# Values of four heads at a time in the first mixer: 512 moving columns in place of 256

## The chip, the cores and the metric

The kernel runs on one core of a Trainium2 chip. The metric is the device time of one execution in microseconds (us); the time before is the median of three runs, 1239.77 us (1239.33 to 1240.48). The program is a two-layer decoder trunk in fp32: a gated linear recurrence (HGRN2) with eight heads, a gated convolutional feed-forward block, a differential attention, a second feed-forward block, over 512 tokens of 1024 features. Only the recurrence, the first fifth of the time, is touched by the change.

Engines are named as in the profile: PE is the matrix engine (PEld its weight loads), DVE the vector engine, ACT the scalar engine, POOL the general one, SP the engine that issues most transfers.

## The reference, cut to what matters

```python
def hgrn2_mixer(h, w_in, w_out, g_norm, lb):
    proj = h @ w_in
    q, f, i, g = jnp.split(proj, ...)          # i: the values, 8 heads of 128
    q = jax.nn.silu(q)
    log_f = jnp.logaddexp(jnp.log(lb), jnp.log1p(-lb) + jax.nn.log_sigmoid(f))
    k = -jnp.expm1(log_f)
...
        o_intra = jnp.einsum('bthk,bshk,btshk,bshv->bthv', qb, kb, decay, vb)
        S_new = jnp.exp(b_last)[..., None] * S + jnp.einsum('bshk,bshv->bhkv', k_dec, vb)
...
    o = rmsnorm(o, g_norm) * jax.nn.silu(g)
    return o @ w_out
```

(The score and value products are written as one here.) The values `i` are a projection of the normed input like q, f and g, and they are needed with tokens on the partitions, 128 tokens in each tile.

## The kernel before, in words

**Products.** Every fp32 product is made of three matmuls of split operands (`mm3`, L97 to L101): high by high, high by low and low by high. A weight tile of 128x1024 is loaded by SP into one of three staging buffers (`stage`, L81), then split: ACT writes the high part (L59), DVE the low part (L60). The parts have three buffers each (`whi`, `wlo`). A projection `proj` onto 128 features takes 24 matmuls: eight slices of the input, three each, with the weights as the stationary operand and 512 tokens moving.

**Values.** The function `value` makes the values of 128 tokens (index j). Here the split input is stationary and the weight columns move. Before the change a call covers two heads: 256 columns, eight slices, three matmuls each. `values(qt)` makes four such calls for head pair qt, from two weight tiles, and writes each result with the row scale into a quarter of the tile `vt` (L332, ACT).

**One head on its way.** `prep` (L339 to L414) turns the f and q projections into scaled queries and keys; its work is on DVE, with copies on ACT. Keys have six buffers, which is one head's worth (`KB`); queries have seven (`QB`), four of them used by a head. `intra` then runs on PE in three pieces:

- scores: small matmuls L424 to L438 of 16 to 80 columns into the banks `pa` and `pb`, and three transposes (L446). The first key of the next head (L347, DVE) reuses the buffer that L424 reads, so it waits for these.
- state: L451, three matmuls with the values.
- output: L491 and L493. L491 needs the masked scores: DVE copies them by masks (L469, the last one is L480), then ACT copies them into place (L483, L486, L488). This chain from the scores to L488 is called the score chain below.

`readout` gates the output with the g projection. Head h's output is "output h" below, its scores are "scores h".

**Order.** The opening `begin` is written out by hand: the f, q and g projections of head 0, then the values of the first two token tiles while the row scales are worked out. The rest of the mixer is ordered by the framework's scheduler, from the loop at the end of `hgrn`: each engine has one fixed list of instructions, which it works off in order. PSUM has four banks `mm` for projections and values, and four banks `at` for the pieces of `intra`.

## Time and profile before

| what | value |
|---|---|
| median of three runs | 1239.77 us (1239.33 to 1240.48) |
| the profiled execution's own time | 1239.78 us |
| its span | 1237.8 us, so 2.0 us lie around it |
| PE busy | 99% of the span |
| DVE busy | 68% of the span, 191.14 us of the 230 us from 20 to 250 us |
| ACT busy | 47% of the span |
| granted PE clock | 1.0 in all stretches of the mixer |

The matmul durations in the profile are from start to modelled end and overlap each other. What a matmul costs in a packed stream is read from the distance of starts: in the stream from 30.15 us to 35.91 us 48 matmuls of 256 columns start, 0.120 us each, though each is listed with 0.28 us. DVE durations overlap by some 0.08 us in the same way.

The scores of heads 0 to 7 start at 46.91, 75.43, 102.07, 124.94, 146.30, 179.19, 200.56 and 221.96 us.

### The profile page before, as it was taken

To read this page: it belongs to the slowest core of one execution; us is meant where nothing else is said; L and a number is where in the kernel's file an instruction comes from. 1 tells how busy PE (TensorE), PEld (TensorE's weight loads), DVE (VectorE), ACT (ScalarE), POOL (GpSimd) and SP (SyncE) were. 2 spreads that over 40 slices of the span, in tenths; PEclk is the share of its full clock that TensorE was granted. 3 is DMA by queue.
4 is the path that set the end of the run, shared out by engine and by line. 5 is a ranking of instruction groups with operands and counts; after the bars stand their busy time and mean duration, and the time that the engine had idled before them with its cause. 6 is when DMAs were issued, how large, how long until landed. Compare 5 with 4: busy or idle time off the path is not lost.

```text
span 1237.8 us, 18004 instructions
## 1 busy us (share of the span) xinstructions
PE 1226.9 (99%) x6994; PEld 1040.4 (84%) x6994; DVE 841.6 (68%) x1643; ACT 578.5 (47%) x1007; POOL 10.1 (1%) x32
## 2 busy tenths in 40 slices
PE   9999999999999999999999999999999999999997
PEld 8888898888888888888888989888888888888887
DVE  7988989587777777633356887877687777762333
ACT  6564555354444444422345666655444444442223
POOL 0000000000000000000000000000000000000001
PEclk9999999999999999999999999999999999999998
DMA  6234232132333333233323322322233333323322
GB/s 233 69 87 122 86 86 57 64 119 86 102 102 91 97 102 90 90 96 100 103 86 116 90 80 75 102 69 86 88 100 102 91 97 102 94 85 97 103 81 69
DMA packets 39613, 117.46 MB, mean 95 GB/s; under 512 B 4280, under 2 KB 10216, under 8 KB 39528
## 3 DMA queue, kind: packets, MB, share of 16 engines
q1 hardware_dynamic: 38488, 115.37, 30.5%
q8 instruction: 55, 0.90, 0.3%
q10 hardware_dynamic: 1040, 0.94, 0.2%
q14 instruction: 30, 0.25, 0.1%
HBM read 112.09 MB, written 3.68 MB: 94 GB/s over the span
## 4 chain that ended last, share of the span: by engine, by line
PE 67%; issue 30%; DVE 1%; ACT 1%; DMA 0%; POOL 0%; SPq 0%; POOLq 0%; ACTq 0%; DVEq 0%
PE mm L99 19%; PE mm L101 19%; PE mm L100 19%; PE po L1021 1%; PE sc L978 1%; PE sc L977 1%; PE tp L1008 1%; PE sc L99 1%; PE sc L100 1%; PE at L491 1%; PE sc L101 1%; PE at L424 1%; PE at L493 0%; PE at L451 0%; DMA raw<-in_w_fqg_dram 0%
## 5 line engine op out<-in xcount | busy, mean ns | idle before, releaser
L99 PE MATMUL mm<-xh,whi 128*128 128x512 f32 x944 | 370.7, 393 | 0.5 <-ACT whi L59 0.4
L100 PE MATMUL mm<-xl,whi 128*128 128x512 f32 x944 | 368.7, 391 | 0.5 <-DVE xl L63 0.5
L101 PE MATMUL mm<-xh,wlo 128*128 128x512 f32 x944 | 367.7, 390 | 0.0
L60 DVE TENSOR_TENSOR wlo<-wst,whi 128x1024 fp32r<-128x1024 f32 (+1 forms) x172 | 206.0, 1200 | 146.1 <-ACT whi L59 144.3
L59 ACT CAST whi<-wst 128x1024 fp32r<-128x1024 f32 (+1 forms) x172 | 177.1, 1033 | 245.8 <-PE mm L100 205.7
L99 PEld LDWEIGHTS mm<-xh,whi 128*128 128x128 f32 x944 | 177.4, 188 | 37.2 <-ACT whi L59 1.1
L101 PEld LDWEIGHTS mm<-xh,wlo 128*128 128x128 f32 x944 | 177.2, 188 | 37.1 <-DVE wlo L60 0.2
L100 PEld LDWEIGHTS mm<-xl,whi 128*128 128x128 f32 x944 | 177.4, 188 | 36.9 <-DVE xl L63 2.0
L99 PE MATMUL mm<-hh,whi 128*128 128x512 f32 (+1 forms) x374 | 141.0, 377 | 0.0
L100 PE MATMUL mm<-hl,whi 128*128 128x512 f32 (+1 forms) x374 | 140.8, 377 | 0.0
L101 PE MATMUL mm<-hh,wlo 128*128 128x512 f32 (+1 forms) x374 | 140.8, 376 | 0.0
L680 DVE TENSOR_TENSOR u<-mm,rbc_f 128x512 f32<-128x512 f32 x88 | 60.2, 688 | 73.1 <-PE mm L101 73.1
L100 PEld LDWEIGHTS mm<-hl,whi 128*128 128x128 f32 x374 | 70.4, 188 | 13.0
L101 PEld LDWEIGHTS mm<-hh,wlo 128*128 128x128 f32 x374 | 70.4, 188 | 13.0
L99 PEld LDWEIGHTS mm<-hh,whi 128*128 128x128 f32 x374 | 70.4, 188 | 12.7
L59 ACT CAST hh<-c 128x512 fp32r<-128x512 f32 x44 | 27.3, 620 | 103.1 <-DVE c L691 103.1
L682 ACT ACTIVATE c<-u,pack 128x512 f32<-128x512 f32 x88 | 71.5, 817 | 8.1 <-DVE u L680 4.3
L99 PE MATMUL mm<-whi,xh 128*128 128x256 f32 x248 | 71.5, 288 | 0.0
L101 PE MATMUL mm<-whi,xl 128*128 128x256 f32 x248 | 70.3, 283 | 0.0
L100 PE MATMUL mm<-wlo,xh 128*128 128x256 f32 x248 | 70.1, 283 | 0.0
L684 DVE SCALAR_TENSOR_TENSOR c<-u,pack,c 128x512 f32<-128x512 f32 x88 | 66.1, 751 | 2.7
L683 DVE SCALAR_TENSOR_TENSOR c<-u,pack,c 128x512 f32<-128x512 f32 x88 | 65.4, 745 | 0.0
(283 smaller groups left out, 1686.3 us busy)
## 6 DMA issues: line engine op xcount, KB each, us to landing
wst<-in_w_up_dram SPq DMA_DIRECT2D x88, 512.0 KB, 3.6
wst<-in_w_down_dram SPq DMA_DIRECT2D x32, 512.0 KB, 3.5
wst<-in_w_fqg_dram SPq DMA_DIRECT2D x21, 512.0 KB, 3.7
wst<-in_w_kq_dram SPq DMA_DIRECT2D x16, 512.0 KB, 3.6
wst<-in_w_down_dram SPq DMA_DIRECT2D x16, 384.0 KB, 3.2
wst<-in_w_i_dram SPq DMA_DIRECT2D x8, 512.0 KB, 4.0
wst<-in_w_ao_dram SPq DMA_DIRECT2D x8, 512.0 KB, 4.5
wst<-in_w_v_dram SPq DMA_DIRECT2D x8, 512.0 KB, 3.7
```

Source lines behind the costliest of these rows:

```text
L59: i = nc.scalar.copy(hi, x)
L60: j = nc.vector.tensor_tensor(lo, x, hi.bitcast(F32), ALU.subtract)
L99: mm(out, s[0], m[0], start=start, stop=False)
L100: mm(out, s[0], m[1], start=False, stop=False)
L101: mm(out, s[1], m[0], start=False, stop=stop)
L424: mm(pa[row, c * P:c * P + 80], ks[1][:, st], r1[:, :, 8 * bk:8 * bk + 8], start=True, stop=True, tile_position=(0, 32 * g))
L491: mm(ch(po, j), vh(j), sct[:, j], start=True, stop=(j == 0))
L680: v.tensor_tensor(u[:, 2:], ps, rb, ALU.mult)
L682: s.activation(c, u[:, 2:], AF.Identity, bias=self.cb[:, layer, n:n + 1], scale=w(2))
L683: v.scalar_tensor_tensor(c, u[:, 1:T + 1], w(1), c, ALU.mult, ALU.add)
L684: v.scalar_tensor_tensor(c, u[:, 0:T], w(0), c, ALU.mult, ALU.add)
L977: mm(sc[c], qs[h][:, c, oi], ks[h][0][:, c, 0:n], start=True, stop=False)
```

## The change

The values are made for four heads at a time. The weights `w_i` are packed in halves of 512 columns instead of quarters of 256, four weight tiles of 128x1024 for a half, so a call of `value` streams 512 columns and fills a whole bank. There are two halves instead of four quarters; `values(half, js)` is called for two token tiles ahead of the `intra` of the head before, and for two after it, at h = 0 and h = 4. The fourth weight tile of a half is split into the buffers `spare`, which before served a later tile alone. Each result has a tile of its own, 128x512, out of six buffers. `begin` stages three value tiles instead of two and the first weights of head 1, and does only the first four input slices of its two token tiles. The query tiles have five buffers instead of seven.

```diff
-KB, QB = 6, 7
+KB, QB = 6, 5
...
-        staged = [self.stage(src) for src in (a["w_i"][0, 0], a["w_i"][0, 1], a["w_fqg"][3])]
+        staged = [self.stage(a["w_i"][0, n]) for n in range(3)]
...
-            nxt = self.weight_split(staged[2])
+            ws.append(self.weight_split(staged[2]))
             values = [self.bank("mm"), self.bank("at")]
-            self.value(values[0], xs, ws, 0, range(KD))
+            self.value(values[0], xs, ws, 0, range(KD // 2))
             rb = self.rows(rc, "n0", "at")
-            self.value(values[1], xs, ws, 1, range(KD))
+            self.value(values[1], xs, ws, 1, range(KD // 2))
...
-            hi, lo = ws[k // 4]
-            c = slice((k % 4) * 256, (k % 4) * 256 + 256)
-            self.mm3(ps[:, :256], (xs[k][0][:, tk], xs[k][1][:, tk]), (hi[:, c], lo[:, c]), k == 0, k == KD - 1)
+            hi, lo = ws[k // 2]
+            c = slice(k % 2 * T, k % 2 * T + T)
+            self.mm3(ps, (xs[k][0][:, tk], xs[k][1][:, tk]), (hi[:, c], lo[:, c]), k == 0, k == KD - 1)
...
+            def values(half, js):
+                if js[0] == 0:
+                    for n in range(len(w_i) % 4, 4):
+                        w_i.append(self.weights(a["w_i"][half, n], tiles=spare if n == 3 else None))
+                for j in js:
+                    begun_j = half == 0 and j < 2
+                    ps = begun[j] if begun_j else self.bank("mm")
+                    self.value(ps, xs, w_i[-4:], j, range(KD // 2 if begun_j else 0, KD))
+                    vt[half, j] = hp.tile([P, T], F32, tag="vt", name="vt", bufs=6)
+                    s.activation(vt[half, j], ps, AF.Identity, scale=rc[:, j:j + 1])
...
-                if h % 2 == 0:
-                    vt[h // 2] = values(h // 2)
+                if h % 4 == 0:
+                    values(h // 4, (0, 1))
                 if h:
-                    o[h - 1] = keep(h - 1, intra(h - 1, vt[(h - 1) // 2], *pr.pop(h - 1)))
+                    o[h - 1] = keep(h - 1, intra(h - 1, *pr.pop(h - 1)))
+                if h % 4 == 0:
+                    values(h // 4, (2, 3))
```

The scheduler's lists change with it, up to the end of the mixer; behind it PE's list is the same as before. Three places matter below.

PE before, at output 0. In a row, the tile left of the arrow is written; right of it stand the moving and the stationary operand. `whi,xh` with 128x256 is a value matmul, `xh,whi` with 128x512 one of a projection.

```order
L99 MATMUL mm<-whi,xh_265 128x256
L100 MATMUL mm<-wlo,xh_265 128x256
L101 MATMUL mm<-whi,xl_266 128x256
L99 MATMUL mm<-whi,xh_143 128x256
L100 MATMUL mm<-wlo,xh_143 128x256
L491 MATMUL at<-scd_394,vt 128x128 x2
L493 MATMUL at<-q_470,S 128x128
...
L101 MATMUL mm<-whi,xl_144 128x256
L99 MATMUL mm<-whi,xh_163 128x256
```

PE now, at the same place:

```order
L101 MATMUL mm<-xh_253,wlo 128x512
L99 MATMUL mm<-xh_265,whi 128x512
L100 MATMUL mm<-xl_266,whi 128x512
L491 MATMUL at<-scd_370,vt 128x128 x2
L493 MATMUL at<-q_446,S 128x128
...
L424 MATMUL at<-r_622,k_616 32x80
L426 MATMUL at<-r_638,k_634 32x48
```

Between scores 0 and output 0 PE had 48 projection matmuls and 26 value matmuls of 256 columns; now it has 71 projection matmuls. The 70 value matmuls that followed output 0 are gone from here, and scores 1 (L424) follow it at once.

DVE before, at the last masked copy (L480) of head 1's scores; `sd` is the masked copy, `F`, `suf`, `tot`, `su` are tiles of `prep` for head 3:

```order
L469 COPY_PREDICATED sd_397<-mask,at 128x4x4
L412 TENSOR_TENSOR tot_910<-tot_902 128x4
L344 TENSOR_SCALAR F<-sf,om,lb 128x512
L480 COPY_PREDICATED sd_397<-mask,at 128x4x16
L364 TENSOR_TENSOR suf<-F 128x128
L365 TENSOR_TENSOR suf<-F,suf 128x128
```

DVE now, at the same place:

```order
L357 TENSOR_TENSOR r_1123<-r_1123,F 128x128
L498 TENSOR_TENSOR ge<-mm,rbc_n_348 128x512
L469 COPY_PREDICATED sd_373<-mask,at 128x4x8
L386 TENSOR_TENSOR su_1146<-tot,su_1146 128x32
L358 TENSOR_TENSOR r_1123<-r_1123,F 128x128
L60 TENSOR_TENSOR wlo<-wst,whi 128x1024
L359 TENSOR_TENSOR r_1123<-r_1123,F 128x128
L469 COPY_PREDICATED sd_373<-mask,at 128x4x4
L387 TENSOR_TENSOR tot_1147<-tot,su_1146 128x32
L501 TENSOR_TENSOR gg<-ge,sg 128x512
L360 TENSOR_TENSOR r_1123<-r_1123,F 128x128
L480 COPY_PREDICATED sd_373<-mask,at 128x4x16
```

Head 3's `prep` up to L387 and a gate (L498, L501) now stand ahead of the last masked copy of head 1. From head 1's L347 up to this L480, DVE's list has 115 rows where it had 99: one more each of L349, L356 to L360, L364 to L366, L385 to L387, L498 and L501, and two more of L354 (one of head 3, and that of head 1, which stood just ahead of L347).

ACT before, in the opening (`rbc` is the tile of row scales, with which the prep of head 0 starts):

```order
L307 ACTIVATE om<-dl 128x8
L59 CAST whi<-wst 128x1024 x2
L332 ACTIVATE vt<-mm,rcol_n_299 128x256
L198 COPY rbc_n_360<-at 128x512
L341 ACTIVATE sf<-fe 128x512
```

ACT now, at the same place:

```order
L307 ACTIVATE om<-dl 128x8
L59 CAST whi<-wst 128x1024 x2
L59 CAST spare_96<-wst 128x1024
L198 COPY rbc_n_348<-at 128x512
L341 ACTIVATE sf<-fe 128x512
```

The split of the fourth value tile stands ahead of the copy of the row scales, where the first eviction of values stood.

More of the change, by code (lines that the diff above doesn't have):

```diff
@@ L272, in begin @@
             proj_tail(2)
-            nxt = self.weight_split(staged[2])
+            ws.append(self.weight_split(staged[2]))
             values = [self.bank("mm"), self.bank("at")]
-            self.value(values[0], xs, ws, 0, range(KD))
+            self.value(values[0], xs, ws, 0, range(KD // 2))
             rb = self.rows(rc, "n0", "at")
-            self.value(values[1], xs, ws, 1, range(KD))
-        return rb, rc, ws, values, nxt
+            self.value(values[1], xs, ws, 1, range(KD // 2))
+        return rb, rc, ws, values
     def value(self, ps, xs, ws, j, ks):
@@ L297, in hgrn @@
             f_ps, q_ps, g_ps = (self.bank() for _ in range(3))
-            rb, rc, w_i, begun, w_f = self.begin(xs, acc, (f_ps, q_ps, g_ps), raw)
+            rb, rc, w_i, begun = self.begin(xs, acc, (f_ps, q_ps, g_ps), raw)
             yt[0] = hp.tile([P, 3, 2, T], F32R, tag="y0", name="y0")
@@ L316, in big, with project @@
                 return hp.tile([P, T], F32, tag=tag, name=name, bufs=bufs)
-            def project(n, w=None):
-                w = w or self.weights(a["w_fqg"][n])
+            def project(n):
+                w = self.weights(a["w_fqg"][n])
                 ps = self.bank("mm")
@@ L322, in project @@
                 return ps
-            def values(qt):
-                ws = w_i if qt == 0 else [self.weights(a["w_i"][qt, n]) for n in range(2)]
-                vt = hp.tile([P, 4, 256], F32, tag="vt", name="vt", bufs=2)
-                for j in range(4):
-                    ps, ks = self.bank("mm") if qt or j > 1 else begun[j], range(KD)
-                    if qt == 0 and j < 2:
-                        ks = ()
-                    self.value(ps, xs, ws, j, ks)
-                    s.activation(vt[:, j], ps[:, :256], AF.Identity, scale=rc[:, j:j + 1])
-                return vt
+            def values(half, js):
[8 more added lines that the diff above has]
+                    s.activation(vt[half, j], ps, AF.Identity, scale=rc[:, j:j + 1])
             def prep(h, f_ps, q_ps):
@@ L415, in prep, with intra @@
                 return r1, r2, qs, ks, tt
-            def intra(h, vt, r1, r2, qs, ks, tt):
+            def intra(h, r1, r2, qs, ks, tt):
                 mm = nc.tensor.matmul
@@ L441, in intra @@
                 ch = lambda t, c: t[:, c * P:(c + 1) * P]
-                vh = lambda j: vt[:, j, (h % 2) * P:(h % 2 + 1) * P]
+                vh = lambda j: vt[h // 4, j][:, h % 4 * P:(h % 4 + 1) * P]
                 q128, k128 = qs[128], ks[128]
@@ L517, in hgrn @@
                 if h:
-                    f_ps, q_ps = project(3 * h, w_f if h == 1 else None), project(3 * h + 1)
+                    f_ps, q_ps = project(3 * h), project(3 * h + 1)
                 pr[h] = prep(h, f_ps, q_ps)
@@ L531, in hgrn @@
             readout(NH - 2, o[NH - 2], gg[0])
-            o[NH - 1] = keep(NH - 1, intra(NH - 1, vt[3], *pr.pop(NH - 1)))
+            o[NH - 1] = keep(NH - 1, intra(NH - 1, *pr.pop(NH - 1)))
             readout(NH - 1, o[NH - 1], gg[1])
@@ L1207, in by_quarter, with by_half @@
     return np.ascontiguousarray(w.reshape(2, 4, P, 4, 256).transpose(3, 0, 2, 1, 4).reshape(4, 2, P, 1024))
+def by_half(w):
+    return np.ascontiguousarray(w.reshape(4, 2, P, 2, T).transpose(3, 0, 2, 1, 4).reshape(2, 4, P, 1024))
 def score_mask():
@@ L1254, in pack @@
         "w_fqg": fqg,
-        "w_i": by_quarter(iv),
+        "w_i": by_half(iv),
         "w_ao": by_tile(i["a_w_out"][0]),
```

## The prediction

> **What bounds the kernel now.** I begin with the head of the page: the span, the busy shares, the granted clock and the chain that ended last.
>
> ```profile
> span 1237.8 us, 18004 instructions
> PE 1226.9 (99%) x6994; PEld 1040.4 (84%) x6994; DVE 841.6 (68%) x1643; ACT 578.5 (47%) x1007; POOL 10.1 (1%) x32
> PEclk9999999999999999999999999999999999999998
> PE 67%; issue 30%; DVE 1%; ACT 1%; DMA 0%; POOL 0%; SPq 0%; POOLq 0%; ACTq 0%; DVEq 0%
> ```
>
> The reader should see one engine in use all the time, at full clock, and a chain that is PE's own work and issue for 97%. So the time is the sum of the distances between PE's starts, plus the few places where PE waits. The change touches the mixer, up to about 250 us, and behind it PE's list is unchanged. The windows (columns: stretch, its length, then PE, PEld, DVE, ACT, POOL busy) narrow it down:
>
> ```profile
> 20.00:250.00 230.00, 229.16 (x2168) 201.02 (x2168) 191.14 (x509) 120.80 (x255) 0.23 (x3) 1.00 0.28 84
> ```
>
> PE is idle for 0.84 us in 230, DVE is busy 83% of it. A change here pays only by fewer PE microseconds, and can lose by making PE wait for DVE.
>
> **Term 1: the columns.** The groups up to 400 us, split by shape, count the value matmuls (one line of the three), and the timeline of PE gives the spacing of starts:
>
> ```profile
> L101 PE MATMUL mm<-whi,xl 128*128 128x256 f32 x120 | 34.1, 284 | 0.0
> L101 PE MATMUL at<-whi,xl 128*128 128x256 f32 x8 | 2.3, 282 | 0.0
> ```
>
> ```profile
> 14.36 0.39 PE L99 MATMUL mm<-xh,whi 128*128 128x512 f32 x1
> ...
> 18.44 0.39 PE L99 MATMUL mm<-xh,whi 128*128 128x512 f32 x1
> ...
> 30.15 0.28 PE L99 MATMUL mm<-whi,xh 128*128 128x256 f32 x1
> ...
> 35.91 0.40 PE L99 MATMUL mm<-xh,whi 128*128 128x512 f32 x1
> 36.15 0.40 PE L100 MATMUL mm<-xl,whi 128*128 128x512 f32 x1
> ...
> 41.38 0.39 PE L99 MATMUL mm<-xh,whi 128*128 128x512 f32 x1
> ```
>
> 128 in each of three lines makes 384 matmuls of 256 columns. From 30.15 to 35.91 us two token tiles' values start, 48 matmuls in 5.76 us: 0.120 us each. For 512 columns, 18 projection matmuls lie between 14.36 and 18.44 us, 0.227 each, and 24 between 35.91 and 41.38, 0.228 each. The change makes 192 matmuls of 512 columns out of the 384, with the same kinds of operand. Before: 384 x 0.120 = 46.1 us. After: 192 x 0.2275 = 43.7 us. **Gain 2.4 us** (2.3 to 2.5 by the two spacings). The listed durations (0.284 against 0.39) would give 34 us, and are the wrong numbers: they overlap. The two spacings fit a fixed part of 12 to 13 ns a matmul, and halving the number of matmuls saves 192 of these.
>
> The Trainium skill ("TensorE: Matmul & The Clock Gate", section "Back-to-back issue gap") gives an isolated gap of N/2.4 + 2.5 ns, that is 109 ns for 256 columns and 216 ns for 512; an estimate by it puts the gain at 0.5 us instead. The trace disagrees at both sizes (120 and 227 ns), so the fixed part is taken from the trace.
>
> **Term 2: the one wait.** All of PE's idle time behind 20 us lies at output 0:
>
> ```profile
> 46.91 0.37 PE L424 MATMUL at<-r,k 128*32 128x80 f32 x8
> ...
> 50.88 0.48 DVE L347 TENSOR_SCALAR k<-sn,om 128x512 f32<-128x512 f32 x1
> ...
> 62.76 0.23 DVE L480 COPY_PREDICATED sd<-mask,at 128x64 f32<-128x64 int32 x1
> ...
> 64.19 0.28 PE L100 MATMUL mm<-wlo,xh 128*128 128x256 f32 x1
> 64.84 0.36 ACT L488 COPY scd<-at 64x256 f32<-64x256 f32 x1
> 65.31 0.68 PE L491 MATMUL at<-scd,vt 128*128 128x128 f32 x4 [0.83 <-issue]
> ...
> 66.86 0.36 PE L101 MATMUL mm<-whi,xl 128*128 128x256 f32 x1
> 67.06 0.28 PE L99 MATMUL mm<-whi,xh 128*128 128x256 f32 x1
> ```
>
> The profile calls the 0.83 us "issue", but L491 starts 0.11 us after ACT's last copy of the scores ended (65.20). PE waited for the score chain: its next start came 1.12 us after the last one instead of 0.12, so the wait cost **1.0 us**. The stretch from scores 0 to output 0 lasted 18.40 us, 17.4 without the wait. The order shows that the 26 value matmuls in it (3.1 us) give way to 23 more projection matmuls (5.2 us), and that eight of the 32 smallest matmuls move ahead (0.2 us): 17.4 - 3.1 + 5.2 - 0.2 = 19.3 us of PE work as cover. The chain needs 18.3 us, and less now, since L354 (1.1 us) no longer stands ahead of L347. The wait goes, 1.0 us gained.
>
> **Term 3: what is late next.** The cover is not thicker everywhere. Output 0 is now followed at once by scores 1, so DVE has to finish heads 1 and 2 sooner. I sum from scores 0 to output 1.
>
> ```profile
> 75.43 0.37 PE L424 MATMUL at<-r,k 128*32 128x80 f32 x8
> ...
> 93.76 0.60 PE L491 MATMUL at<-scd,vt 128*128 128x128 f32 x4
> ...
> 120.79 0.36 ACT L488 COPY scd<-at 64x256 f32<-64x256 f32 x1
> 121.37 0.61 PE L491 MATMUL at<-scd,vt 128*128 128x128 f32 x4
> ```
>
> ```profile
> 50.90:89.20 38.30, 33.71 (x101) 1.00 0.24 69
> ```
>
> ```profile
> L354 DVE TENSOR_TENSOR r<-qe,sq__1224 128x512 f32<-128x512 f32 x1 | 1.1, 1079 | 0.0
> ...
> L356 DVE TENSOR_TENSOR r<-r,F 128x256 f32<-128x256 f32 x8 | 5.3, 662 | 0.1
> ...
> L349 DVE TENSOR_TENSOR qe<-mm,rbc_n 128x512 f32<-128x512 f32 x8 | 5.5, 683 | 0.0
> L498 DVE TENSOR_TENSOR ge<-mm,rbc_n 128x512 f32<-128x512 f32 x8 | 5.5, 690 | 0.0
> L501 DVE TENSOR_TENSOR gg<-ge,sg 128x512 f32<-128x512 f32 x8 | 5.7, 718 | 0.0
> ...
> L360 DVE TENSOR_TENSOR r<-r,F 128x128 f32<-128x128 f32 x8 | 3.1, 389 | 0.1
> L387 DVE TENSOR_TENSOR tot<-tot,su 128x32 f32<-128x32 f32 x8 | 1.7, 210 | 0.2
> ```
>
> PE: 19.3 us to output 0, 1.55 us for the output itself (65.31 to 66.86), then scores 1 to output 1. That took 18.33 us (75.43 to 93.76) with 66 projection matmuls and will hold 96, of them 30 new: 18.33 + 30 x 0.228 = 25.2. Together 46.0 us.
>
> DVE: before, head 1's L347 started 3.97 us behind scores 0; without L354 ahead of it 2.9. From there to head 1's L480 DVE was busy 33.7 us (the window). The list now has 16 more instructions: two L354 (2.2), L356 (0.66), four of 0.39 (like L360), three more of the same 128x128 size (1.2), three of 0.21 (like L387), and L349, L498, L501 (2.1), 8.3 us by durations. They overlap by some 0.08 us each, so 7.0 to 8.3; I take 7.6. Then 2.4 us of copies (62.76 to 65.20): 2.9 + 33.7 + 7.6 + 2.4 = 46.6 us. DVE is late by 0.6 us, if it is never idle on the way; were L347 to start as soon as its operands allow, nearer 2.5 us, it is nearly in time. Between no wait and the 4.6 us by which this stretch was longer than its busy time before (38.3 - 33.7), the sum is nearest to the low end: **a wait of 0.5 us** at output 1. Of the later outputs, 2, 3, 6 and 7 lose 1 to 4 us of cover by the order. Output 2 had the least to spare (0.22 us, 121.15 to 121.37); it loses 1.0 us, but head 3's prep, which DVE did in between, now lies earlier (at output 1, the rows above). I cost them at nothing, and leave up to two waits of 1.0 us for them to a rival.
>
> **Edits that cost nothing, and their cover.** Weight traffic stays at eight value tiles of 512 KB, moved in SP's list, and splits stay at eight. The fourth tile's split now stands ahead of the row scales on ACT:
>
> ```profile
> 22.65 4.94 SPq L81 DMA_DIRECT2D wst<-in_w_fqg_dram  x3
> ...
> 27.05 0.47 ACT L332 ACTIVATE vt<-mm,rcol_n 128x256 f32<-128x256 f32 x1 [2.02 <-PE mm L101]
> 27.49 0.59 ACT L198 COPY rbc_n<-at 128x512 f32<-128x512 f32 x1
> 28.11 0.69 DVE L339 TENSOR_TENSOR fe<-mm,rbc_n 128x512 f32<-128x512 f32 x1 [0.88 <-ACT rbc_n L198]
> ```
>
> ```profile
> wst<-in_w_fqg_dram SPq DMA_DIRECT2D x3, 512.0 KB, 3.4
> ```
>
> The staging buffer is free at 22.65 us, the data land 3.4 us after issue, near 26.5, and both splits are done by 29 (1.0 on ACT, 1.2 on DVE). The eviction at 27.05 us followed the first 24 value matmuls (2.9 us), so the values begin near 24 us; PE wants the new tile after 31 of the wide ones, 7 us on, near 31. The prep of head 0, delayed by 1 us (L339 at 28.11), has 96 x 0.2275 = 21.8 us of value matmuls as cover, where it had 11.5. If the tile landed 4 us late, PE would wait some 1 to 2 us for head 1's weights. Evictions of values become 8 of 512 columns in place of 16 at 0.47 us on ACT, which is idle half the time. Fewer query buffers add no wait that the keys do not have: six key buffers hold one head, so DVE may not pass L347 before the scores of the head ahead are done, and by then the query tile that is now wanted, from two heads back, has been read. Breaks between long and short matmuls cost some 0.1 us on each side (66.86 to 67.06 is 0.20 instead of 0.12); three are added and four or so go: nothing.
>
> **Sum.** 1239.78 (the profiled execution, 0.01 above the median) - 2.4 - 1.0 + 0.5 = **1236.9 us**.
>
> **Rivals.**
>
> *Waits come back.* DVE's list grows just ahead of output 1, and each time DVE waits for ACT's half of a split in that stretch PE pays in full; outputs 2, 3, 6 and 7 have less cover. For it: sums within 1 us of each other. Against: PE has waited at one output of eight so far. Half a wait to two waits of 1.0 us, the size at output 0, beyond the forecast: 1237.4 to 1238.9.
>
> *The columns give little.* If a value matmul of 512 columns with the input stationary took up to 0.240, the largest spacing in the packed rows above (35.91 to 36.15), the fixed part that is saved shrinks from 13 ns to nothing, and term 1 with it: 46.1 - 192 x 0.240 = 0 at the end, 1239.3. Against it: 0.227 in long streams. The Trainium skill's section named above is this rival with a fixed part of 2.5 ns; an estimate by it gives 1238.8.
>
> *Slower: splits of weights stall the chain on DVE.* The value weights of a half hold all three `whi` pairs, so the next projections' splits come in a bunch, when a half's last matmuls release them, and DVE works in order.
>
> ```profile
> L60 DVE TENSOR_TENSOR wlo<-wst,whi 128x1024 fp32r<-128x1024 f32 x34 | 41.7, 1230 | 17.3 <-ACT whi L59 17.3
> ...
> 75.18 1.22 DVE L60 TENSOR_TENSOR wlo<-wst,whi 128x1024 fp32r<-128x1024 f32 x1 [2.51 <-ACT whi L59]
> ```
>
> DVE already sits 17.3 us ahead of 34 splits, up to 2.5 us at once here, so far where nobody waits. If three such waits of 2.5 us fell into the stretch from scores 0 to output 1, PE would wait 0.5 + 7.5 us there: 1244.4. Slower by 0.2% (1242.3) it is from 5.9 us of waits in all. Against it: the splits of this stretch take buffers that are free a projection earlier, by the order.
>
> **How the numbers follow.** A measurement of this kernel can tell about 0.2%, 2.5 us, from no change: the border is 1237.3. Chances: the forecast, 1236.3 to 1237.3, 50%; waits come back 32%; columns give little 5%; slower 7%; better than the forecast, down to 1236.0 (no wait at output 1, and the 0.227 spacing) 6%. So faster 56%, same 37%, slower 7%. The range leaves out the slower case and the best end: 1236.1 to 1239.3.
>
> **What would show it.** Right: in the changed trace, value matmuls start 0.227 to 0.229 us apart; output 0 starts within 0.25 us of the matmul before it; the idle time ahead of L491 shows at head 1, below 1 us; everything behind the mixer keeps its length. Wrong: spacing of 0.24; idle time of PE ahead of L491 or L99 above 1.5 us in sum; the row scales' copy later than 29 us. The forecast falls if the DVE list holds more idle time from scores 0 to output 1 than I allowed.

## The result, and the profile after

The changed kernel takes **1248.0 us** (median of six runs, 1245.59 to 1250.24) against 1239.63 us of the kernel before in the same session (six runs, 1239.29 to 1240.48). The ratio is 1.0066, 95% interval 1.0056 to 1.0076. So it is slower by 8.4 us, where I had forecast 1236.9 us and a range up to 1239.3. The profiled execution took 1250.24 us, 10.5 us more than the one of before.

Behind the mixer's code the lines have moved by two (L545 is now L547). The head of the page after:

```profile
span 1248.4 us, 17609 instructions
PE 1230.7 (99%) x6802; PEld 1033.9 (83%) x6802; DVE 841.3 (67%) x1643; ACT 576.7 (46%) x999; POOL 10.1 (1%) x32
PE 58%; issue 31%; DVE 8%; ACT 2%; DMA 0%; POOL 0%; SPq 0%; POOLq 0%; ACTq 0%; DVEq 0%
```

DVE now has 8% of the chain that ended last, where it had 1%. The forty slices of PEclk on the page show the same digits before and after, since they cut off after tenths. The waits of PE up to 330 us (columns: total, times, longest) name the places:

```profile
PE at L491 <- ACT scd L488: 3.9, 2, 3.5
PE mm L99 <- DVE res L547: 2.9, 1, 2.9
PE at L451 <- ACT kt L448: 1.0, 1, 1.0
```

And the timeline of PE has them in order:

```profile
198.32 0.39 PE L99 MATMUL mm<-xh,whi 128*128 128x512 f32 x1
199.19 0.71 PE L491 MATMUL at<-scd,vt 128*128 128x128 f32 x4 [0.48 <-ACT scd L488]
...
208.37 0.39 PE L100 MATMUL mm<-xl,whi 128*128 128x512 f32 x1
209.74 0.94 PE L451 MATMUL at<-vt,kt 128*128 128x128 f32 x6 [0.98 <-ACT kt L448]
...
219.38 0.39 PE L101 MATMUL mm<-xh,wlo 128*128 128x512 f32 x1
223.24 0.71 PE L491 MATMUL at<-scd,vt 128*128 128x128 f32 x4 [3.47 <-ACT scd L488]
...
276.25 0.39 PE L101 MATMUL mm<-y,wlo 128*128 128x512 f32 x1
279.50 0.76 PE L99 MATMUL mm<-xh,whi 128*128 128x512 f32 x1 [2.86 <-DVE res L547]
280.06 0.63 PE L100 MATMUL mm<-xl,whi 128*128 128x512 f32 x1
280.48 0.63 PE L101 MATMUL mm<-xh,wlo 128*128 128x512 f32 x1
```

The number in brackets counts from the modelled end of the matmul before. What a wait costs is the distance of starts less the usual 0.227: 0.64 us at output 5, 1.14 at state 6, 3.63 at output 6, 3.02 at the first up-projection behind the mixer. Waits in heads 5 and 6 cost 5.4 us, the one behind the mixer 3.0.

Behind the last two waits the matmuls are slower as well: 280.06 to 280.48 is 0.42 instead of 0.227. Windows around them (the last three columns: granted clock, DMA share, GB/s) show why:

```profile
224.00:228.00 4.00, 4.00 (x118) 3.77 (x118) 4.00 (x6) 2.41 (x4) 0.00 (x0) 0.57 0.64 190
...
276.00:279.00 3.00, 0.63 (x3) 0.19 (x1) 2.18 (x4) 2.19 (x3) 0.00 (x0) 0.96 0.45 168
279.00:286.00 7.00, 6.50 (x16) 5.14 (x17) 3.57 (x6) 1.24 (x2) 0.00 (x0) 0.53 0.27 75
```

Windows of one microsecond show either full or half clock: 0.50 from 281 to 282 us, 1.00 from 230 to 231 us. With these two values, the mean of 0.57 over 4.0 us is 3.4 us at half, and the two rows at 279 are 0.2 + 6.6 = 6.8 us at half. In matmuls, 14 distances from 279.50 on take 6.10 us where 14 x 0.2275 = 3.2 do: 2.9 us lost there. From output 6 to the transposes of head 7 it took 5.54 us (223.24 to 228.78), and 3.99 at full clock in e1 below (223.11 to 227.10): 1.5 us lost.

The sum of the profiled execution: - 2.4 (columns) - 1.0 (output 0) + 5.4 + 3.0 + 2.9 + 1.5 = + 9.4 of 10.5 us. Most of the rest is in the opening. Up to the transposes of head 0 the change moves 96 x (0.2275 - 0.120) = 10.3 us of value work, and they come 11.2 us later (49.22 and 60.45): 16 of head 0's small matmuls now cut into a projection, with breaks.

### The profile page after: what moved, and what is told of

The parts are those of the page before. It is cut to its first block, busy times and chain, and to the rows that moved or that the text cites. A ratio compares the mean times of both kernels' runs of the same rounds, so it can differ in the third digit from the quotient of the medians.

```text
span 1248.4 us, 17609 instructions
## 1 busy us (share of the span) xinstructions
PE 1230.7 (99%) x6802; PEld 1033.9 (83%) x6802; DVE 841.3 (67%) x1643; ACT 576.7 (46%) x999; POOL 10.1 (1%) x32
## 4 chain that ended last, share of the span: by engine, by line
PE 58%; issue 31%; DVE 8%; ACT 2%; DMA 0%; POOL 0%; SPq 0%; POOLq 0%; ACTq 0%; DVEq 0%
PE mm L99 16%; PE mm L101 16%; PE mm L100 16%; PE po L1023 1%; DVE wlo L60 1%; DVE sd L469 1%; PE sc L980 1%; PE sc L979 1%; PE tp L1010 1%; ACT whi L59 1%; PE sc L99 1%; PE sc L100 1%; PE sc L101 1%; PE at L99 0%; PE at L101 0%
## 5 line engine op out<-in xcount | busy, mean ns | idle before, releaser
L99 PE MATMUL mm<-xh,whi 128*128 128x512 f32 x944 | 372.0, 394 | 3.2 <-DVE res L547 2.9
L60 DVE TENSOR_TENSOR wlo<-wst,whi 128x1024 fp32r<-128x1024 f32 x170 | 203.3, 1200 | 145.1 <-ACT whi L59 143.1
L59 ACT CAST whi<-wst 128x1024 fp32r<-128x1024 f32 x170 | 174.8, 1033 | 259.5 <-PE mm L100 220.1
L99 PEld LDWEIGHTS mm<-xh,whi 128*128 128x128 f32 x944 | 178.1, 189 | 40.5 <-ACT sq L143 3.3
L99 PE MATMUL mm<-hh,whi 128*128 128x512 f32 (+1 forms) x374 | 141.0, 377 | 0.0
L99 PEld LDWEIGHTS mm<-hh,whi 128*128 128x128 f32 x374 | 70.4, 188 | 13.0
L691 ACT ACTIVATE c<-c 128x512 f32<-128x512 f32 x44 | 27.8, 632 | 75.2 <-DVE c L686 75.2
L99 PE MATMUL mm<-whi,xh 128*128 128x256 f32 (+1 forms) x170 | 53.8, 317 | 0.0
L100 PE MATMUL mm<-wlo,xh 128*128 128x256 f32 (+1 forms) x170 | 52.6, 309 | 0.0
```

The source lines that it names most:

```text
L59: i = nc.scalar.copy(hi, x)
L60: j = nc.vector.tensor_tensor(lo, x, hi.bitcast(F32), ALU.subtract)
L99: mm(out, s[0], m[0], start=start, stop=False)
L100: mm(out, s[0], m[1], start=False, stop=False)
L691: s.activation(cg, cg, AF.Silu)
```

## The experiments

All times are medians in us, each beside runs of the kernel before in the same session (1239.5 to 1239.8). "e1" is the base of most others.

| run | what | us | ratio to before, 95% |
|---|---|---|---|
| e1 | changed, banks exchanged | 1244.07 | 1.0033 [1.0021, 1.0046] |
| e2 | before, banks made to collide | 1243.67 | 1.0030 [1.0019, 1.0042] |
| e3 | before, five query buffers | 1239.68 | 0.9998 [0.9989, 1.0007] |
| e4 | changed, value matmuls in halves | 1250.39 | 1.0084 [1.0070, 1.0098] |
| e5 | e1, gates' product on POOL | 1241.79 | 1.0015 [1.0007, 1.0024] |
| e6 | e1, late splits on POOL | 1244.88 | 1.0040 [1.0028, 1.0053] |
| e7 | e1, second half in pairs | 1245.32 | 1.0046 [1.0032, 1.0059] |
| e8 | e1, second half one head later | 1246.72 | 1.0056 [1.0043, 1.0069] |
| e9 | e1, scores 0 early | 1244.32 | 1.0040 [1.0028, 1.0053] |
| e10 | e9 and e5 | 1241.95 | 1.0021 [1.0012, 1.0029] |
| e11 | before, gates' product on POOL | 1242.38 | 1.0024 [1.0015, 1.0033] |
| e12 | e5, running sum on POOL too | 1246.06 | 1.0053 [1.0040, 1.0066] |
| e13 | e1, one split held back on ACT | 1242.64 | 1.0023 [1.0014, 1.0031] |
| e14 | e1, 7 key and 4 query buffers | 1239.97 | 1.0004 [0.9995, 1.0013] |
| e15 | e1, gates' product left out | 1238.90 | 0.9994 [0.9985, 1.0003] |
| e16 | before, 7 key and 6 query buffers | 1239.39 | 0.9998 [0.9989, 1.0007] |
| e17 | e14, two products on ACT | **1238.11** | 0.9985 [0.9976, 0.9994] |
| e18 | e16, two products on ACT | 1239.35 | 0.9997 [0.9988, 1.0006] |

### The wait behind the mixer: a PSUM bank (e1, e2)

PE's list behind the mixer is the same as before, so the wait had to come from something that the list doesn't show. The addresses in the built programs do: the banks of the last four tiles of the output projection, and that of the first up-projection behind them.

```
kernel    tiles 4, 5, 6, 7     first up-projection
before    0, 3, 2, 1           0
changed   1, 3, 2, 0           0
e1        5, 7, 6, 4           0
e2        3, 2, 1, 0           0
```

Which bank a tile gets follows from the order in which banks are asked for and come free in the scheduler's plan; e1 and e2 permute them by asking for one bank more or fewer. Before, bank 0 was that of tile 4, read long ago. Now it is that of tile 7, and the first up-projection waits until DVE has read it. DVE's reading of the last tile, in the changed kernel and in the one before:

```profile
278.66 0.68 DVE L547 TENSOR_TENSOR res<-mm,rbc_o 128x512 f32<-128x512 f32 x1
```

```profile
274.06 0.68 DVE L545 TENSOR_TENSOR res<-mm,rbc_o 128x512 f32<-128x512 f32 x1
```

In the changed kernel PE starts 0.16 us after this read has ended (279.34, 279.50). Before, PE had started that product at 271.85, 2.2 us ahead of the read.

e1 exchanges the banks of the two groups, without any other change in the four engines' lists; e2 gives the kernel before the same collision (with PE's order changed only among products of the output projection):

```diff
-            spare = [hp.tile([P, 1024], F32R, tag=f"spare{i}", name=f"spare{i}") for i in range(2)]
+            spare = [hp.tile([P, 1024], F32R, tag=f"spare{i}", name=f"spare{i}") for i in range(2)]; self.bank("at")
```

```diff
-                          extra=[self.bank("at") for _ in range(2)])
+                          extra=[self.bank("at") for _ in range(1)])
```

> The changed kernel with the PSUM banks of the mixer's two groups exchanged (one unused bank of the second group is asked for first), so that the last output tile of the mixer lies in bank 4 instead of bank 0, the bank that the first up-projection of the feed-forward block takes. Every engine's list is the same. Theory bank: the 3.0 us wait ahead of the first L99 behind the mixer goes, and the 14 matmuls behind it start 0.228 apart instead of 0.427 (2.8 us): 1248.0 - 5.8 = 1242.2 us. Rival late: the wait is for the mixer's end, which comes late for another reason than the bank: 1248.0. Rival clock: the wait goes, but the low rate belongs to the earlier wait at output 6 and stays: 1245.0.

> The kernel before, with one bank fewer of the second group for the mixer's first output tiles, which puts its last output tile into bank 0, the first up-projection's (in the kernel before it is in bank 1). PE's order changes only among products of the output projection; DVE's and ACT's lists are the same. Theory bank: a wait of some 3 us ahead of the first L99 behind the mixer and a low rate behind it, 1239.6 + 3.0 + 2.8 = 1245.4 us. Rival: the bank has no part in it, 1239.6.

PE's waits in e1, then in e2 (without one of 0.3 and 0.2 us that both share with the changed kernel):

```profile
PE at L491 <- ACT scd L488: 3.8, 2, 3.4
PE at L451 <- ACT kt L448: 0.9, 1, 0.9
```

```profile
PE mm L99 <- DVE res L545: 2.9, 1, 2.9
PE at L491 <- issue: 0.8, 1, 0.8
```

In e1 the wait is gone and the kernel is 3.9 us faster than the changed one; in e2 the same wait of 2.9 us stands in the kernel before, which is 3.9 us slower. The cause is shown both ways. Part of each median is the clock: at the same mean granted clock, 0.998, the fastest execution of e1 (1242.35 us) lies 3.2 us below the fastest of the changed kernel (1245.59), close to the wait's 3.0. Both fall short of the 5.8 us that I expected, because the low clock does not follow every such wait: in the profiled executions of e1 and e2 it stayed at 1.00, even behind e1's 3.35 us at output 6.

### Columns and query buffers (e3, e4)

```diff
-KB, QB = 6, 7
+KB, QB = 6, 5
```

> The kernel before with five query buffers instead of seven, nothing else; every engine's list is the same, only waits can differ. Theory of the prediction: the query buffers cost nothing, 1239.6 us (within 0.5). Rival: DVE waits for query tiles in the late heads and so is late at outputs 5 and 6, 1241 to 1244.

```diff
-            self.mm3(ps, (xs[k][0][:, tk], xs[k][1][:, tk]), (hi[:, c], lo[:, c]), k == 0, k == KD - 1)
+            n = 0
+            for s, m in ((0, hi), (0, lo), (1, hi)):
+                for e in ((0, 512),) if k + n == 0 else ((0, 256), (256, 512)):
+                    n += 1
+                    self.nc.tensor.matmul(ps[:, e[0]:e[1]], xs[k][s][:, tk], m[:, c.start + e[0]:c.start + e[1]],
+                                          start=k + n == 1, stop=k == KD - 1 and n == 6)
```

> The changed kernel with each value matmul of 512 columns issued as two of 256 (but for the first of each tile): 376 of 256 and 8 of 512 in place of 192 of 512. Theory of term 1 (0.120 against 0.2275 us): 184 x 0.0125 = 2.3 us more, 1250.3 us, the waits of heads 5 and 6 as they are, since no value matmul lies there. Rival with a fixed part of 2.5 ns a matmul: 0.5 us more, 1248.5. If the waits shrink because PE is later: 1248.

The query buffers cost the kernel before nothing (1239.68 beside 1239.80, by the times alone); the changed kernel without its five was not tried, but e14 below gets faster with four. The halves cost 2.4 us, as term 1 had it; with the run to run spread of this kernel that alone would be weak, but the trace has it too. In the changed kernel 48 value matmuls in a row start from the first to the second of these rows, 47 distances of 0.2266 us; the step to the third, a shorter matmul, is a break of 0.32:

```profile
35.42 0.39 PE L99 MATMUL mm<-whi,xh 128*128 128x512 f32 x1
...
46.07 0.39 PE L101 MATMUL mm<-spare,xl 128*128 128x512 f32 x1
46.39 0.34 PE L424 MATMUL at<-r,k 128*32 128x80 f32 x4
```

In e4 a tile of one wide matmul and 46 halves takes 5.75 us (36.17 to 41.92), 0.120 us a half, against 24 x 0.2266 = 5.44. So the columns' gain is real: 0.31 us on each of eight tiles, 2.5 us in all.

### The waits at heads 5 and 6: whose are they? (e5 to e16)

First what the traces say. Head 7's first key (L347) needs head 6's scores to be done, since it reuses their buffer; DVE then copies by masks up to L480, and ACT copies on. The last transposes of scores 6 (PE L446), and DVE's L347 and L480, before and after:

```profile
202.82 0.55 PE L446 MATMUL at<-pack,k 128*128 128x128 f32 x3
203.26 0.48 DVE L347 TENSOR_SCALAR k<-sn,om 128x512 f32<-128x512 f32 x1
215.20 0.24 DVE L480 COPY_PREDICATED sd<-mask,at 128x64 f32<-128x64 int32 x1
```

```profile
203.21 0.55 PE L446 MATMUL at<-pack,k 128*128 128x128 f32 x3
207.31 0.48 DVE L347 TENSOR_SCALAR k<-sn,om 128x512 f32<-128x512 f32 x1
218.89 0.23 DVE L480 COPY_PREDICATED sd<-mask,at 128x64 f32<-128x64 int32 x1
```

Before, DVE waits for the scores and begins 0.44 us behind the start of the transposes. After, it is 4.1 us behind, and L480 ends 3.7 us later. It did not get slower: it had more to do between the two keys. One instruction a head, L354 (the first step of the queries), marks where a head's queries are made. Before:

```profile
171.84 1.12 DVE L354 TENSOR_TENSOR r<-qe,sq__2196 128x512 f32<-128x512 f32 x1
181.89 0.48 DVE L347 TENSOR_SCALAR k<-sn,om 128x512 f32<-128x512 f32 x1
...
203.26 0.48 DVE L347 TENSOR_SCALAR k<-sn,om 128x512 f32<-128x512 f32 x1
203.98 1.18 DVE L354 TENSOR_TENSOR r<-qe,sq__2598 128x512 f32<-128x512 f32 x1
```

After:

```profile
180.55 0.48 DVE L347 TENSOR_SCALAR k<-sn,om 128x512 f32<-128x512 f32 x1
183.45 1.08 DVE L354 TENSOR_TENSOR r<-qe,sq__2105 128x512 f32<-128x512 f32 x1
203.68 1.08 DVE L354 TENSOR_TENSOR r<-qe,sq__2390 128x512 f32<-128x512 f32 x1
207.31 0.48 DVE L347 TENSOR_SCALAR k<-sn,om 128x512 f32<-128x512 f32 x1
```

The stretch between the keys of heads 6 and 7 held none of the two heads' query steps before, and now holds both. Before, head 6's were made from 171.84 us on, in the long stretch from scores 4 to scores 5 (146.30 to 179.19 us), where PE worked through the 96 value matmuls for heads 6 and 7. In the changed kernel the last value matmul lies ahead of output 3. The windows from scores 5 to 6 and 6 to 7 of the kernel before, then from scores 4 to 5, 5 to 6 and 6 to 7 of e1 (the lists of the changed kernel; columns: length, then PE, PEld, DVE, ACT, POOL busy) show what that leaves:

```profile
179.19:200.56 21.37, 21.37 (x216) 18.11 (x215) 18.73 (x50) 12.40 (x29) 0.00 (x0) 1.00 0.33 89
200.56:221.96 21.40, 21.40 (x217) 18.11 (x216) 20.12 (x54) 12.70 (x29) 0.13 (x2) 1.00 0.22 66
```

```profile
155.22:176.59 21.37, 21.37 (x216) 18.10 (x215) 19.80 (x56) 12.07 (x27) 0.00 (x0) 1.00 0.23 72
176.59:200.93 24.34, 23.88 (x227) 20.06 (x226) 22.88 (x62) 13.14 (x29) 0.00 (x0) 1.00 0.29 87
200.93:224.87 23.94, 19.65 (x207) 16.22 (x206) 22.63 (x60) 12.90 (x29) 0.00 (x0) 1.00 0.25 74
```

In the last one DVE has 22.6 us of work and PE 19.7, where before it was 20.1 and 21.4.

The second contribution is on ACT. After L480 (its end is at 219.12) ACT still has the splits of two late weight tiles in front of the score copies (L483). It comes to them late itself: ahead of them stands a cast of y (218.54 us), for which ACT waited 2.43 us until DVE had written y.

```profile
219.07 1.05 ACT L59 CAST whi<-wst 128x1024 fp32r<-128x1024 f32 x1
220.12 1.04 ACT L59 CAST spare<-wst 128x1024 fp32r<-128x1024 f32 x1
221.07 1.21 ACT L483 COPY scd<-sd 32x128 f32<-32x128 f32 x4
```

**POOL as a relief (e5, e6, e11, e12).** Three tries to unload DVE or ACT onto the idle engine, and the same relief in the kernel before:

```diff
-                v.tensor_tensor(gg, ge, sg, ALU.mult)
+                nc.gpsimd.tensor_tensor(gg, ge, sg, ALU.mult)
```

(e5, and e11 on the kernel before.)

> The kernel of e1 (changed kernel, banks exchanged) with the gates' product (L501, 0.72 us a head on DVE) made by POOL. Theory DVE: in heads 4 to 6 DVE has more work than PE gives cover, so three products off its list take 2.2 us from the 5.2 us of waits at outputs 5, 6 and state 6, and the rest of what is left is at output 6: 1244.1 - 2.2, or 1241.9 us, less where the low clock does not follow. Rival ACT: the waits come from the weight splits on ACT ahead of the score copies, and stay: 1244.1. Rival POOL: it slows DVE or is late itself, over 1245.

> The kernel before with the gates' product on POOL, the same relief as e5's. It has one wait, 1.0 us at output 0. Theory: with value matmuls spread over the heads the kernel before is not short of DVE time, so the relief brings at most that wait: 1238.8 to 1239.8 us. Rival: DVE paces the kernel before as well, and PE has idle time that the profile does not show: below 1238.

```diff
-            items = [(banks[n], self.weights(w_src[n], tiles=late[n])) for n in range(n0)]
+            items = []
+            for n in range(n0):
+                st, (hi, lo) = self.stage(w_src[n]), late[n] or self.weight_tiles()
+                self.nc.gpsimd.tensor_copy(hi, st)
+                v.tensor_tensor(lo, st, hi.bitcast(F32), ALU.subtract)
+                items.append((banks[n], (hi, lo)))
```

> The kernel of e1 with the high parts of the mixer's first four output weights (L59 in the late tiles) written by POOL instead of ACT; at output 6 that takes two splits, 1.9 us, from ahead of the score copies on ACT, and puts one more split of y (0.68 us) ahead of L480 on DVE. Theory ACT: output 6's wait of 3.4 us becomes 1.5 to 2.2, 1242.2 to 1242.9 us. Rival, DVE alone: L480 ends it, the wait stays or grows by 0.7: 1244.1 to 1244.8.

e12, in `keep`:

```diff
-                self.sq_add(oacc, po, h == 0)
+                if h:
+                    sq = self.sp.tile([P, T], F32, tag="sq", name="sq", bufs=2)
+                    s.activation(sq, po, AF.Square)
+                    nc.gpsimd.tensor_tensor(oacc, oacc, sq, ALU.add)
+                else:
+                    self.sq_add(oacc, po, True)
```

> e5 with the running sum of squares (L144, 0.69 us a head on DVE) on POOL as well. Theory DVE: at outputs 5 and 6 another 0.7 us each comes off the chain, the waits there go from 0.96 and 1.23 to 0.3 and 0.5 us: 1240.4 us. Rival ACT: what is left at these outputs is the copies on ACT behind the last copy by a mask, 1241.8 as e5.

e5's time came out as theory DVE had it (1241.8), but for another reason. One product of POOL in e5 and the DVE instruction beside it:

```profile
98.87 2.31 POOL L501 TENSOR_TENSOR gg<-ge,sg 128x512 f32<-128x512 f32 x1 [64.23 <-ACT sg L499]
```

```profile
100.00 1.22 DVE L387 TENSOR_TENSOR tot<-tot,su 128x32 f32<-128x32 f32 x1
```

The mean of L387 in e1 is 0.21 us. Seven of POOL's eight products have one such DVE instruction beside them, which took 0.8 to 1.1 us longer than its like in e1 and ended up to 0.55 us behind POOL's (at the eighth DVE waited for POOL itself). Together that is 6.6 us. DVE lost 5.5 us of work and was busy 1.1 us longer (189.4 us in e1, 190.6 in e5, from 20 to 250 us). From the start of scores 6 to the end of L480 DVE gained only 0.6 us (18.15 us in e1, 17.51 in e5); the other 1.6 us came from ACT, whose new order had no split ahead of the score copies. e11 and e12 say the same: the relief makes the kernel before 2.9 us slower, and more of it makes e5 4.3 us slower. e6, no faster than e1 where theory ACT had it 1.2 to 1.9 us faster, is confounded: ACT's two splits went, but L480 came 2.1 us later, with a split of y ahead of it and L347 at 1.26 us beside POOL's cast (0.48 in e1).

**Where the value matmuls lie (e7, e8), and an earlier start (e9, e10).**

```diff
-                if h % 4 == 0:
+                if h in (0, 5):
                     values(h // 4, (0, 1))
+                if h == 5:
+                    values(1, (2, 3))
...
-                if h % 4 == 0:
-                    values(h // 4, (2, 3))
+                if h == 0:
+                    values(0, (2, 3))
```

(e8, with all four token tiles at h = 5.) And e7, where values(2, ...) and values(3, ...) work as in the kernel before, with 256 columns:

```diff
-                if h % 4 == 0:
-                    values(h // 4, (0, 1))
+                if h in (0, 4, 6):
+                    values(h // 2, (0, 1))
...
-                if h % 4 == 0:
-                    values(h // 4, (2, 3))
+                if h == 0:
+                    values(0, (2, 3))
```

> The kernel of e1 with the values of heads 0 to 3 made at a time (512 columns) and those of heads 4, 5 and of heads 6, 7 in pairs (256 columns) where the kernel before makes them. Theory cover: the value matmuls at heads 4 and 6 give back the cover, no wait at heads 5 and 6, and half of the columns' gain stays: 1239.8 - 1.0 (output 0) - 1.2 = 1237.6 us. Rival: the waits are not a matter of where value matmuls lie, 1242 or more.

> The kernel of e1 with the values of heads 4 to 7 made one head later (at h = 5 instead of h = 4, all four token tiles ahead of the products of head 4). By the order 55 of the 96 wide value matmuls then lie behind scores 3 instead of 5, 12.5 us of PE work moved one head on. Theory cover: the wait at output 5 goes and the one at output 6 shrinks to below 1 us, 1239 to 1240 us. Rival: the work is only moved and DVE's backlog at head 6 is the same, 1244.

In both the waits at outputs 5 and 6 and at state 6 are gone. In e8 head 7's first key is 1.4 us behind the transposes where it was 4.1 (215.53, 214.16), and in e7 it is 0.25 us ahead of them (208.70, 208.95), so DVE is in time there as in the kernel before. So the place of the value matmuls decides how late DVE is there. But the time was not won: the rivals' times came out, though not their reason. PE's waits in e8:

```profile
PE at L491 <- ACT scd L488: 2.4, 1, 2.4
PE mm L99 <- ACT whi L59: 2.0, 1, 2.0
PE mm L100 <- DVE y L60: 0.9, 1, 0.9
```

The L491 here is output 7; e7 waits at the same three places for 2.4, 1.5 and 0.9 us. With the values later, the scheduler pulled other projections forward: 36 of the 192 matmuls of the output projection start ahead of scores 7 in e7 and e8, where e1 has none. In e8 those pulled ahead of output 6 wait for weights that ACT has not split yet (2.0 us at 220.57), and output 6 then starts just behind its last copy (230.49, 230.55). The waits moved on to the mixer's end. My 1237.6 and 1239 to 1240 were wrong by as much.

```diff
-                if h % 4 == 0:
-                    values(h // 4, (2, 3))
...
+                if h == 0:
+                    values(0, (2,))
+                    sc0 = score(0, *pr.pop(0))
+                    values(0, (3,))
+                elif h == 4:
+                    values(1, (2, 3))
```

(`score` is the first part of `intra`, up to the transposes and their copy.)

> The kernel of e1 with the scores and transposes of head 0 issued ahead of the last token tile's values (in e1 they stand behind all values of the half and behind 48 projection matmuls, at 58.4 us, while head 0's scores could start at 42.5, and DVE is busy 5.55 of the 12.02 us ahead of 58.4). Theory early idle: what DVE loses there is what it lacks at heads 5 and 6; some 4 us of head 0's copies by masks move into the idle time, the waits shrink from 5.2 us to about 1: 1239 to 1240 us. Rival, late bunching: DVE's lateness at head 6 comes from the order within heads 5 and 6 and not from earlier work, 1243 to 1244.

> e9 and e5 together: head 0's scores early, and the gates' product on POOL. If both give DVE time, the waits at heads 5 to 7 are below 1 us in all: 1239.8 - 2.4 - 1.0 + 0.5 to 1.0 = 1237 us (1236.5 to 1238.5), below the kernel before. If e5's rest (3.2 us of waits) has another cause than DVE's lateness, 1241 to 1242.

This theory falls: e9 is as slow as e1, with 3.37 us at output 6 again, and e10 as slow as e5. DVE time gained at head 0 is not there at head 6: L347 of head 7 is 3.9 us behind the transposes (207.54, 203.68), as it was 4.1 in e1. That fits the key buffers, which hold one head and so bound how far DVE can be ahead.

**ACT alone, buffers alone, DVE alone (e13 to e16).**

```diff
                 s.copy(sct[0:64, :, 64:128], pb[0:64, 192:448].rearrange("p (c o) -> p c o", c=4))
+                if h == NH - 2:
+                    s.copy(spare[0][0:64, 0:64], sct[0:64, 0, 64:128])
```

> The kernel of e1 with a copy of 64x64 (its values are not used) into the spare weight tile behind head 6's last score copy, which holds the split of that tile (L59, 1.03 us) behind the score copies on ACT. PE's list is the same and DVE's up to output 6. Theory ACT: the wait at output 6 shrinks by the 0.94 us that ACT spends on it, from 3.35 to 2.4 us, 1243.1 us against e1's 1244.1 (less where the low clock depends on the wait's length). Rival DVE alone: 3.35 stays.

The cleanest of the runs: PE's list is the same and ACT's differs in this split. Its ACT rows:

```profile
219.01 1.05 ACT L59 CAST whi<-wst 128x1024 fp32r<-128x1024 f32 x1
219.96 1.21 ACT L483 COPY scd<-sd 32x128 f32<-32x128 f32 x4
```

The wait at output 6 fell from 3.35 to 2.40 us, by the 0.95 us of the split, and the median by 1.4, of which the fastest executions, both at a mean clock of 0.998, show 0.8 (1242.35 and 1241.59). By the same measure both splits are an estimated 1.9 us of the 3.35, and DVE's lateness is the rest; only the one was tried.

```diff
-KB, QB = 6, 5
+KB, QB = 7, 4
```

(e14; e16 has 7, 6 in place of 6, 7 in the kernel before.)

> The kernel of e1 with seven key and four query buffers (six and five). Theory lead: head h + 1's first key no longer waits for scores h, DVE may be one key further ahead, and its lateness at heads 5 and 6 (1.7 and 4.1 us from the end of the scores to L347) falls; the waits shrink from 5.2 to 1 to 2 us, 1239 to 1240.5 us. Rival: DVE lacks time in these heads, not buffers, 1244; with four query buffers it may even wait more.

```diff
-                gg = big("gg", "gg", 2)
-                v.tensor_tensor(gg, ge, sg, ALU.mult)
-                return gg
+                return ge
```

(e15)

> The kernel of e1 with the gates' product left out (L501: the output is gated by g itself and not by g times its sigmoid), so DVE has 0.7 us a head less and POOL nothing. Theory DVE: up to output 6 some 2 us come off the chain in heads 4 to 6: waits of 3 us in place of 5.2, 1241.5 to 1242 us. If DVE's time is not what counts: 1244.

> The kernel before with seven key and six query buffers (six and seven). Theory lead: only its wait of 1.0 us at output 0 can go: 1238.6 to 1239.6 us. If more than 1.5 us faster, the kernel before was short of key buffers too.

One key buffer more lets L347 of head 7 start at 200.40 us in e14, ahead of scores 6 (200.58), and L480 ends 17.4 us behind the start of these scores (18.15 in e1). Two waits are left, and no split stands ahead of them on ACT:

```profile
PE at L491 <- ACT scd L488: 2.5, 2, 1.3
```

That gains 4.1 us on e1, by the earlier key and by the new order on ACT together. The kernel before stays where it was with the same buffer (e16: 0.3 us less, within the interval, and its wait at output 0 is still there). Taking 0.7 us a head off DVE without POOL gains 5.2 us on e1 (e15), more than I expected of it; wait time left there is 0.3 and 1.25 us. That too is not DVE alone: at output 6 both splits of weights now stand elsewhere than just ahead of the score copies, while L480 ends 17.9 us behind the start of scores 6, only 0.3 less than in e1.

**A version that beats both (e17, e18).**

```diff
-                v.tensor_scalar(F, sf, om[:, h:h + 1], lb[:, h:h + 1], ALU.mult, ALU.add)
+                s.activation(F, sf, AF.Identity, bias=lb[:, h:h + 1], scale=om[:, h:h + 1])
...
-                v.tensor_scalar(ks[1], sn, om[:, h:h + 1], None, ALU.mult)
+                s.activation(ks[1], sn, AF.Identity, scale=om[:, h:h + 1])
```

> The kernel of e14 (changed kernel, banks exchanged, seven key and four query buffers) with two of DVE's products by a constant for each feature written by ACT: F (L344, 0.55 us) and the first key (L347, 0.48 us). DVE has 1.0 us a head less, ACT some 1.2 us more and is busy 12.5 of 21.4 us there. Theory DVE: the waits of 2.5 us at outputs 5 and 6 go, 1240.0 - 2.5 = 1237.5 us, or to 1236.5 with the small breaks around them. Rival: ACT is late in its turn, or the rest is latency between the engines and not DVE's time, 1239.5 to 1241.

> The kernel before with the same two products on ACT and seven key and six query buffers (e16 with the relief of e17). If the values' columns are what e17 gains, this stays 2.4 us above e17: 1238.7 to 1239.4 us (its one wait, 1.0 us at output 0, goes). If the relief itself is the gain, the two are equal.

e17 takes 1238.11 us, 1.6 us less than the kernel before beside it, with one wait left in the mixer, 0.84 us at output 6. The same relief leaves the kernel before where it was (1239.35), with its wait of 0.8 us at output 0. The slowest execution of e17 (1238.27) is faster than the fastest of e18 (1238.91). So the change, with its banks and buffers set right, is worth 1.2 us between the two. One wait of about 1.0 us stands in each, so half of the 2.4 us is lost elsewhere, in the opening by the starts that follow; no run changes the opening alone. The transposes of head 0 start at 49.03 us in e18 and at 60.60 in e17, 11.6 us later where the moved value work is 10.3.

## Why the prediction was wrong

- **Term 1, the columns: right.** 0.2266 us a matmul of 512 columns against 0.2275 assumed, and 0.120 for 256; e4 gives the gain back. The estimate from the Trainium skill's gap of N/2.4 + 2.5 ns (a gain of 0.5 us) is refuted at 0.120 and 0.2266.
- **Term 2, the wait at output 0: right.** Output 0 starts at 77.65 us, 0.23 behind the matmul before it.
- **Term 3, a wait of 0.5 us at output 1: wrong by its size.** There is none; the score copies end at 103.56 us, output 1 starts at 104.43. DVE needed 1.4 us less, net, than my sum of rows.
- **"Of the later outputs, 2, 3, 6 and 7 lose 1 to 4 us of cover by the order ... I cost them at nothing": this step failed.** It cost 5.4 us at outputs 5, 6 and state 6 (with the splits of the next point), and output 5 was not on my list. I compared each output's cover within its own head. What counts there is how far ahead DVE is when the head begins, and that is made one or two heads earlier, in the head that holds the value matmuls. Before, such heads came every second time; after, heads 4 to 7 in a row hold none, and DVE's work from scores 5 to 6 and 6 to 7 grew by 4.2 and 2.5 us, to 22.9 and 22.6, against 23.9 and 19.7 of PE. e7 (values in pairs again, and DVE in time for head 7) and e8 (less late with the values one head later) show that their place decides this. e14 and e15 have smaller waits with a buffer more or with less DVE work, in part by ACT's order, which changed with them; e9 shows that time won at head 0 does not help.
- **"Edits that cost nothing": the splits stay at eight, but their place was not priced.** I had looked at splits on ACT only at the row scales. The two splits ahead of the score copies at output 6 cost an estimated 1.9 of the 5.4 us (e13 shows one of them at 0.95). My slower rival named splits and DVE, but from scores 0 to output 1, where nothing happened. Breaks between long and short matmuls, put at nothing there too, leave the opening 0.9 us longer than the moved work (11.2 against 10.3 us).
- **"Everything behind the mixer keeps its length": failed.** PE's list there is the same, and I took that for the same time. Banks are given out in an order that the list does not show; the collision costs 3.0 us (e1, e2).
- **Low clock: not thought of.** 4.4 us of the profiled execution. It follows waits of 2 us and more in some executions, and makes most of the spread: 1245.6 us at a mean granted clock of 0.998 to 1250.2 at 0.993 for the changed kernel, 1239.6 to 1241.1 for e14, whose longest wait is 1.35 us.
- My mark for being wrong, idle time of PE above 1.5 us ahead of L491 or L99, came true: 6.8 us.

## What to carry to other kernels

Work on the bound engine that is "also cover" must be counted as cover where it stood: list, head by head, how far the second engine is ahead when the head begins, and ask which heads in a row will lack the work that is moved away. An unchanged instruction list is not unchanged time: compare the PSUM banks (or any buffer that a plan gives out) at the seam to the next stage. A relief for a busy engine is best taken to one that does not disturb it (ACT here, not POOL), and the order of splits on ACT can cost as much as DVE's lateness (1.9 of 3.35 us at output 6, by the estimate from e13).

## What the runs showed of the hardware

**Half clock in lumps of 3.4 us.** Behind waits of PE the granted clock fell to one half for about 3.4 us or twice that (the windows of the changed kernel above), not in every execution and not in step with the wait's length. e1 kept 1.00 behind 3.35 us of idle time; e8 lost it behind a wait of 2.0 us:

```profile
221.00:225.00 4.00, 4.00 (x12) 3.11 (x11) 4.00 (x12) 1.85 (x4) 0.00 (x0) 0.57 0.01 5
```

Again 0.57 over 4 us, so 3.4 us at half, 1.7 us lost. The Trainium skill ("TensorE: Matmul & The Clock Gate", section "Part 1: The HAM clock gate") has a gate that is either full or half and is set by windows of about 3.4 us that run freely, not in step with the kernel. The trace agrees with the two values (0.50 and 1.00 in windows of one microsecond), with the length, and with a fall that comes in some executions only; it disagrees with a whole idle window as the condition, since the fall followed 2.0 us of waiting in e8 and 2.4 in e13.

**POOL holds up DVE.** Beside seven of the eight products of POOL in e5 one DVE instruction, whatever its size, took 0.8 to 1.1 us longer and ended with POOL's product or up to 0.55 us behind it: L387 of 128x32 took 1.22 us against 0.21 in e1, L356 of 128x256 1.67 against 0.64. The Trainium skill ("GPSIMD Engine Reference", section "1. Specifications") says that the two engines share SBUF interfaces and contend where DVE reads two SBUF inputs or is in a 2-port perf mode. The seven rows agree, all with two inputs from SBUF. Two rows go beyond that condition. In e6 L347, with one tile as input, took 1.26 us beside a cast of POOL, and no run here shows in which mode it ran. And L60, with two inputs, ran at its usual 1.2 us beside the first 0.4 to 0.9 us of POOL's products.
